# A hybrid decoder block on one core: the up-projection's first group prepares its inputs product by product

## The chip, the cores and the metric

The kernel runs on one core of a Trainium2 chip. A core has five engines, each with its own queue that it works off in order: TensorE for matrix products (PE, and PEld for its weight loads), VectorE (DVE), ScalarE (ACT), GpSimd (POOL) and SyncE (SP), which here only issues DMAs. The metric is the device time of one execution in microseconds (us). The number given is the median of three runs; the profile is of one further execution.

## The reference

The reference is one decoder layer on a sequence of 2048 tokens with width 1024, in float32. It is computed as follows.

```
n    = rms_norm(x, attn_norm_w)
proj = n @ w_in              # q, k, v, gate, a, b of DeltaNet; q, k, v, gate of retention
o    = concat(gated_deltanet(...), retention(...))      # 4 + 4 heads of 128
h    = x + o @ w_out
n2   = rms_norm(h, mlp_norm_w)
hdn  = causal_dwconv3(n2 @ w_up)                        # 1024 -> 2 * 2816
g, u = split(hdn)
h    = h + (silu(g) * u) @ w_down                       # 2816 -> 1024
out  = rms_norm(h, final_norm_w)
```

The DeltaNet heads carry a state from chunk to chunk, so that part is a chain of small matrix products, each waiting for a step on VectorE. The three big projections (w_out, w_up, w_down) have no such chain.

## The kernel before, in words

**Number format.** Every float32 matrix that is multiplied in a big projection is split into a rounded high part and the rest. `split` (L1123) does it in two instructions: an ACT copy into the rounded format (L1124) and a VectorE subtraction for the rest (L1125). `mm3` then makes one product out of three matmuls (L118, L119, L120): high by high, high by low, low by high.

**Seven products.** The projections use a scheme of the Strassen family: both operands are cut into 2 x 2 blocks, and seven block products numbered 1 to 7 take the place of eight. Four of the seven need a sum or difference of blocks on each side. In the up-projection the blocks of the input are b11, b12, b21, b22, and the products are used in the order 1, 2, 6, 7, 5, 4, 3. Product 1 takes b11, product 2 takes b21, product 3 takes b22; products 5, 6, 7 and 4 take the differences t1 = b12 - b11, t2 = b22 - t1, t3 = b22 - b12 and t4 = b21 - t2.

**Batches and passes.** The mixers (normalisation, input projection, DeltaNet, retention, output projection) work in four batches of 512 tokens, numbered 0 to 3. The up-projection works in two passes q = 0 and q = 1, each over two batches (1024 tokens); a pass goes through 22 groups g of output columns. Pass 0 reads the normalised rows n2d of batches 0 and 1 only, which lie in DRAM long before batch 3 is done. The up-projection is a generator (`mlp_up`, L1115 on). For q = 0 it loads the first group's weights (`load_w`, L1157, DMA at L1169, into the tiles "wur"; sums at L1176, splits into the tiles "wu"), then prepares the inputs (`prep_x`, L1130), then runs `group` (L1190) and, one group ahead, `load_w` of the next. `prep_x` takes one k tile at a time: it loads two rows of blocks into two raw tiles "xr" (L1138), makes four differences into "st" (L1146), and splits all seven operands into the tiles "x", before it goes to the next of the four k tiles. A product of a group is 4 k tiles x 3 matmuls = 12 matmuls of 128 x 512 (tile "p"), followed by an addition out of PSUM into "uc" (L1206 on VectorE, or a copy, L1226 and L1228 on ACT). `tail` does the convolution, the activation and the differences for the down-projection.

**What sets the order.** `ORDER` is a list of stage names written out by hand. A name begins with the batch; the rest says which stage: `pro` normalisation, `a`, `f`, `k0`, `q0`, `v0`, `kq` input projections, `dec` decays, `c`, `d`, `e`, `b`, `l` the preparation of DeltaNet chunks, `r00` to `r13` the recurrence (first digit the pair of heads, second the chunk; steps at L860 to L886), `h` and `y` retention, `P` products of the gate, `g` and `G` the gated mixing (L578 to L588), `W1` to `W7` the products of the output projection (weights "wv", loaded at L1061; the residual input "wx", L1045), and `N` the second normalisation (L1103), which writes n2d. A name that begins with `U` advances the up-projection's generator by one `yield`; the number behind the U has no meaning. Names of one stage may stand between those of another, so that their instructions mix. From this traced order the framework makes a fixed queue for each engine at compile time: at each point of a modelled run the engine takes the earliest traced instruction that is ready. The numbers of buffers per tile name (NXR, NUC, BUFS and others) limit how many of a name live at once.

**Fences.** `fence(k)` (L1127) puts the DMAs inside it, in the queue of SP, behind a certain earlier DMA: the last load of mixer weights ("c"), a load of batch 3's DeltaNet base ("z"), or a load of "wx" in batch 3 ("x"). Which one is read from a table, and where the named DMA has not been traced yet it is "c":

```
FX = (0, 2, 4, 1, 5)
FENCE = ["c", ("z", NB - 1, 0), ("z", NB - 1, 1), ("x", NB - 1, 0, 0), ("x", NB - 1, 1, 0), ("x", NB - 1, 2, 0), ("x", NB - 1, 3, 0)]
return tc.issue_after(marks.get(FENCE[FX[k]], marks["c"]).ins)
```

The first four entries of FX are for the input loads of the four k tiles, the fifth for the first group's weights.

## Time and profile before

| | before |
|---|---|
| runs, us | 2439.99, 2438.68, 2437.32 |
| median, us | 2438.68 |
| profiled execution, us | 2446.21 |
| its span, us | 2444.4 |
| TensorE busy in the span, us | 2389.4 |
| VectorE, ScalarE, GpSimd busy, us | 1658.3, 1075.1, 412.4 |
| mean granted TensorE clock | 0.991 |

The span reaches from the first to the last instruction of the profiled execution; the time is that of the whole execution. In lines of the profile, L and a number is a line of the kernel, `out<-in` names the tiles an instruction writes and reads, `x` and a number counts instructions, and a bracket at the end of a line gives how long the engine was idle before it and what ended that idle time. A granted clock of 1.00 is full speed.

### The profile page before, as it was taken

The numbers are of one execution on the slowest core, as the hardware profiler recorded it, in microseconds if no ns is written. First come the engines' busy times: TensorE is split into PE (matmuls) and PEld (weight loads), VectorE is DVE, ScalarE is ACT, GpSimd is POOL, SyncE is SP. The second block draws the span as 40 slices with busy tenths as digits, with TensorE's granted clock in tenths as the row PEclk, the third lists the DMA queues.
The fourth block names the chain that finished last, engine by engine and source line by source line (L and its number), as shares of the span: only waits on it lengthen the run. The fifth ranks groups of instructions, "written<-read, shape, count | busy, mean of one in ns | idle before, by whom it ended". The sixth has DMA issues, their size and how long they took to land.

```text
span 2444.4 us, 35994 instructions
## 1 busy us (share of the span) xinstructions
PE 2389.4 (98%) x12404; PEld 2010.2 (82%) x12404; DVE 1658.3 (68%) x3187; ACT 1075.1 (44%) x2286; POOL 412.4 (17%) x753
## 2 busy tenths in 40 slices
PE   8999899999999999998999999999999999999998
PEld 7887788878887888887788888888888888888887
DVE  6865686664744872667989988995556576554673
ACT  6744555555443662456544434442222234332341
POOL 1154113520043103140000000000000002431030
PEclk9999999999999999999999999999999999999999
DMA  8955789886777865697998878777668578774782
GB/s 317 379 195 181 290 316 357 309 335 229 277 265 223 321 234 173 208 339 272 351 343 320 301 283 311 290 261 255 241 229 319 198 272 281 251 223 144 229 253 99
DMA packets 307142, 652.40 MB, mean 267 GB/s; under 512 B 51024, under 2 KB 130320, under 8 KB 306960
## 3 DMA queue, kind: packets, MB, share of 16 engines
q1 hardware_dynamic: 290240, 635.80, 73.5%
q10 hardware_dynamic: 16720, 14.30, 1.9%
q8 instruction: 98, 1.61, 0.3%
q14 instruction: 84, 0.69, 0.1%
HBM read 444.12 MB, written 205.88 MB: 266 GB/s over the span
## 4 chain that ended last, share of the span: by engine, by line
PE 86%; DMA 4%; DVE 4%; POOL 3%; issue 2%; ACT 1%; SPq 0%; ACTq 0%; POOLq 0%; DVEq 0%
PE p L118 11%; PE p L119 11%; PE p L120 11%; PE d L120 6%; PE d L118 6%; PE d L119 6%; PE tok L539 3%; PE tok L540 3%; PE tok L541 3%; PE chm L119 3%; PE chm L118 3%; PE chm L120 3%; PE wo L120 2%; PE wo L118 2%; PE wo L119 2%
## 5 line engine op out<-in xcount | busy, mean ns | idle before, releaser
L119 PE MATMUL p<-x,wu 128*128 128x512 f32 x1176 | 457.8, 389 | 0.8 <-DVE x L1125 0.8
L118 PE MATMUL p<-x,wu 128*128 128x512 f32 x1176 | 452.8, 390 | 1.7 <-ACT uc L1226 1.3
L120 PE MATMUL p<-x,wu 128*128 128x512 f32 x1176 | 450.4, 389 | 0.0
L118 PEld LDWEIGHTS p<-x,wu 128*128 128x128 f32 x1176 | 220.7, 188 | 49.0 <-ACT uc L1226 1.7
L119 PEld LDWEIGHTS p<-x,wu 128*128 128x128 f32 x1176 | 220.7, 188 | 47.3 <-DVE x L1125 1.7
L120 PEld LDWEIGHTS p<-x,wu 128*128 128x128 f32 x1176 | 220.7, 188 | 45.8
L1253 DVE SCALAR_TENSOR_TENSOR acc<-uc,base,acc 128x1022 f32<-128x1022 f32 (+1 forms) x176 | 220.9, 1278 | 37.1 <-ACT acc L1250 36.9
L1206 DVE TENSOR_TENSOR uc<-p,uc 128x512 f32<-128x512 f32 x224 | 152.8, 685 | 135.1 <-PE p L120 129.6
L539 PE MATMUL tok<-wc,n 128*128 128x512 f32 (+2 forms) x576 | 196.9, 352 | 8.1 <-ACT n L449 5.7
L540 PE MATMUL tok<-wc,n 128*128 128x512 f32 (+2 forms) x576 | 200.2, 349 | 0.0
L541 PE MATMUL tok<-wc,n 128*128 128x512 f32 (+2 forms) x576 | 196.5, 349 | 3.1 <-DVE n L452 3.1
L184 POOL TENSOR_TENSOR vt<-vr 128x512 f32<-128x512 f32 x44 | 72.1, 1642 | 636.3 <-DMA vr<-in_w_d 458.9
L119 PE MATMUL d<-v,uu 128*128 128x512 f32 x448 | 174.3, 389 | 0.0
L120 PE MATMUL d<-v,uu 128*128 128x512 f32 x448 | 174.3, 389 | 0.0
L118 PE MATMUL d<-v,uu 128*128 128x512 f32 x448 | 174.3, 389 | 0.0
L118 PE MATMUL chm<-n,wc 128*128 128x512 f32 x384 | 153.1, 399 | 1.8 <-ACT og L583 1.8
L119 PE MATMUL chm<-n,wc 128*128 128x512 f32 x384 | 151.4, 394 | 0.0
L120 PE MATMUL chm<-n,wc 128*128 128x512 f32 x384 | 150.8, 393 | 0.0
L1250 ACT ACTIVATE acc<-uc,base 128x1024 f32<-128x1024 f32 x88 | 97.3, 1144 | 97.5 <-DVE uc L1206 49.5
L539 PEld LDWEIGHTS tok<-wc,n 128*128 128x128 f32 x576 | 109.8, 192 | 21.4 <-ACT n L449 5.9
L408 DVE SCALAR_TENSOR_TENSOR ca<-ca,base 128x511 f32<-128x511 f32 (+2 forms) x144 | 110.6, 768 | 21.6 <-ACT ca L405 21.1
L541 PEld LDWEIGHTS tok<-wc,n 128*128 128x128 f32 x576 | 108.6, 192 | 15.7 <-DVE n L452 3.3
(280 smaller groups left out, 5049.2 us busy)
## 6 DMA issues: line engine op xcount, KB each, us to landing
wu<-wu SPq DMA_DIRECT2D x308, 512.0 KB, 5.5
wc<-wd SPq DMA_DIRECT2D x116, 512.0 KB, 5.3
wv<-kW SPq DMA_DIRECT2D x112, 512.0 KB, 6.6
wc<-kP SPq DMA_DIRECT2D x84, 512.0 KB, 6.3
ur<-au SPq DMA_DIRECT2D x56, 512.0 KB, 5.7
wd<-wc SPq DMA_DIRECT2D x44, 512.0 KB, 6.6
wur<-in_w_u SPq DMA_DIRECT2D x44, 512.0 KB, 6.2
au<-st SPq DMA_DIRECT2D x88, 256.0 KB, 5.0
```

The costliest lines, as they stand in the source:

```text
L118: PE.matmul(ps, ah, bh, start=(first and i == 0), stop=False, skip_group_check=chk)
L119: PE.matmul(ps, ah, bl, start=False, stop=False, skip_group_check=chk)
L120: PE.matmul(ps, al, bh, start=False, stop=(i == n - 1), skip_group_check=chk)
L184: POOL.tensor_tensor(tt[:, j], a, b_, op=ALU.subtract)
L408: DVE.scalar_tensor_tensor(acc[:, s:], ps[:, :TB - s], w, acc[:, s:], op0=ALU.mult, op1=ALU.add)
L539: PE.matmul(ps, ah, wh, start=(k == 0), stop=False)
L540: PE.matmul(ps, ah, wl, start=False, stop=False)
L541: PE.matmul(ps, al_, wh, start=False, stop=(k == KT - 1))
L1206: add = lambda o, ps, a: DVE.tensor_tensor(o, ps, a, op=ALU.add)
L1250: ACT.activation(acc, u, AF.Copy, scale=mcw[:, ci, 2:3])
L1253: DVE.scalar_tensor_tensor(acc[:, t:], u[:, :T2 - t], w, acc[:, t:], op0=ALU.mult, op1=ALU.add)
```

## The change

The change has three parts.

First, for pass 0 the preparation of the inputs goes product by product. `first_x` loads all raw tiles, k tile by k tile, and splits the operand of product 1 only. `more_x(i)` prepares the operand of product i for all four k tiles; it writes t1 and t3 and t4 over raw blocks that are not needed any more, and t2 into "st". In the first group, `group` calls `more_x` for the next product ahead of each product, with a `yield` after each preparation and each product. Pass 1 keeps `prep_x`.

Second, with these yields the up-projection's first group takes 18 entries of the order instead of 11. The first of them moves from behind 3W3 to ahead of 3r10, and the others are spread between the entries of batch 3. A dozen other entries of the order move by one to three places.

Third, buffer numbers change: NUC 5 to 4, NPR 9 to 10, NXR 7 to 8, and in BUFS kv 8 to 7, NT 7 to 5, Cw 4 to 3, wvt 9 to 8, ca 11 to 12, rk 13 to 14, rq 2 to 4, rv 10 to 11.

```diff
@@ -21,7 +21,7 @@
 NVV = 23
 NWUR = 2
 NST = 4
-NUC = 5
+NUC = 4
 NACC = 8
 NWU = 9
 NWV = 5
@@ -29,27 +29,28 @@
 NU = 4
 NPB = 9
 NPM = 4
-NPR = 9
+NPR = 10
 NRAW = 3
 NLATE = 4
-NXR = 7
+NXR = 8
 FD = 6
-BUFS = {"n1": 8, "ykq": 4, "kv": 8, "NT": 7, "AT": 10, "o": 6, "n2s": 15, "xk": 2, "og": 1, "co": 6, "Cw": 4,
-        "wx": 1, "wsq": 5, "wvr": 2, "wvt": 9, "ca": 11, "mix": 5, "D": 6, "rk": 13, "rq": 2, "rv": 10, "sm": 5,
+BUFS = {"n1": 8, "ykq": 4, "kv": 7, "NT": 5, "AT": 10, "o": 6, "n2s": 15, "xk": 2, "og": 1, "co": 6, "Cw": 3,
+        "wx": 1, "wsq": 5, "wvr": 2, "wvt": 8, "ca": 12, "mix": 5, "D": 6, "rk": 14, "rq": 4, "rv": 11, "sm": 5,
         "sc": 15, "wg": 2, "kt": 4, "Ar": 2, "Nb": 6, "rot": 1, "rrow": 5}
 
-ORDER = ("0pro 0k0 0dec 0v0 0q0 0d0 0a0 0a1 0c0 0f0 0d1 0a2 0c1 0f1 0b0 0e0 0d2 0e1 0c2 0h0 0y0 0h1 0f2 "
-         "0d3 0a3 0c3 0l0 0e2 0O0 0y1 0f3 0r00 0r01 0e3 0r02 0r03 0O2 0kq 0b1 0l1 0O1 0r10 0r11 0p0 1pro "
-         "0O3 0h2 0Q0 0r12 0y2 0p1 0g0 1k0 0r13 0h3 0G0 1a0 0y3 0g1 1dec 0G1 1a3 1f0 1d0 1c0 1q0 0W1 0W2 "
-         "0W6 1d1 1a1 0W7 1f1 1c1 0W5 1v0 1e1 1d3 0Q2 0Q1 0W3 1f3 1d2 1b0 1h1 1e0 0Q3 1a2 0W4 1c3 1c2 1f2 "
+ORDER = ("0pro 0k0 0v0 0dec 0q0 0d0 0a0 0a1 0c0 0f0 0d1 0a2 0c1 0f1 0b0 0e0 0d2 0e1 0c2 0h0 0y0 0h1 0f2 "
+         "0d3 0a3 0c3 0l0 0O0 0y1 0f3 0r00 0e2 0r01 0e3 0r02 0r03 0O2 0kq 0b1 0l1 0O1 0r10 0r11 0p0 1pro "
+         "0O3 0h2 0Q0 0r12 0y2 0p1 0g0 1k0 0r13 0h3 0G0 0y3 1a0 0g1 1dec 0G1 1a3 1f0 1d0 1c0 1q0 0W1 0W2 "
+         "0W6 1d1 1a1 1c1 0W7 1f1 0W5 1v0 1e1 1d3 0Q2 0Q1 0W3 1f3 1d2 1b0 1h1 1e0 0Q3 1a2 0W4 1c3 1c2 1f2 "
          "1e2 1y1 1h0 1l0 1y0 1e3 0N 1r00 1r01 1b1 1r02 1S 1kq 1P1 1h2 1y2 1l1 1r03 1h3 1P4 1T 1P6 1P7 "
-         "1r10 1y3 1P5 1r11 2pro 1r12 2k0 1g1 1g0 2v0 1r13 1G1 2dec 1G0 2a0 2d1 1W1 1W2 2d0 2c0 2f0 1W6 "
-         "2a2 1W7 2d2 1W5 2f2 2c2 2a1 1W3 2e2 2e0 1W4 2c1 2f1 2q0 2d3 2e1 2b0 2a3 2h1 2y1 2c3 2b1 2h0 2f3 "
+         "1r10 1y3 2pro 1P5 1r11 1r12 2k0 1g1 1g0 2v0 1r13 1G1 2dec 1G0 2a0 2d1 1W1 1W2 2d0 2c0 2f0 1W6 "
+         "2a2 1W7 2d2 1W5 2f2 2a1 2c2 1W3 2e2 2e0 1W4 2d3 2c1 2f1 2q0 2a3 2e1 2b0 2h1 2y1 2c3 2b1 2h0 2f3 "
          "2e3 2l0 2P1 2r00 1N 2S 2kq 2r01 2P4 2T 2P6 2y0 2l1 2P7 2r02 2r10 2h2 2y2 2P5 2h3 3pro 2r03 2r11 "
          "2r12 3k0 2y3 2r13 2g1 2g0 3a0 3f0 2G0 3dec 3a1 2G1 3d0 2W1 2W2 3a2 3d1 2W6 3q0 3f1 3c1 2W7 3c0 "
-         "3e1 3b0 3d3 3v0 3h0 3e0 3y0 3h1 3d2 3c2 3y1 3kq 3f2 2W5 3a3 3e2 3c3 3f3 2W3 3b1 3l0 3e3 3S 3P1 "
-         "3r00 3r01 3P4 3h2 3T 3P6 3P7 3r02 3y2 3h3 3P5 3r03 3l1 3g0 3r10 3G0 3r11 3r12 3y3 2W4 2N 3g1 "
-         "3W1 3r13 3W2 3G1 3W6 3W7 3W5 3W3 U1 U2 U3 U4 3W4 3N U0 U6 U9 U7 U8 U5 U10")
+         "3e1 3b0 3d3 3v0 3h0 3d2 3e0 3y0 3h1 3c2 3y1 3kq 3f2 2W5 3e2 3a3 3c3 3f3 2W3 3b1 3l0 3e3 3S 3r00 "
+         "3r01 3P1 3P4 3h2 3T 3P6 3P7 3r02 3P5 3y2 3h3 3r03 3l1 3g0 U3 U1 U2 U4 3r10 3G0 3r11 U0 3r12 2W4 "
+         "U6 3y3 3g1 2N U7 U8 3W1 3r13 3W2 U9 3G1 3W6 3W7 3W5 3W4 3W3 U13 U17 U15 3N U12 U16 U5 U10 U11 "
+         "U14")
 P = 128
 S = 2048
 D = 1024
@@ -1154,6 +1155,47 @@
                 split(x_, src)
             yield
 
+    raws, t2s = {}, {}
+
+    def x_part(xc, i, kt, src):
+        x_ = xc[i, kt] = unit(xp, f"x{i}_{kt}", [P, 2, TB], F32R, bufs=1)
+        split(x_, src)
+
+    def first_x(xc):
+        for kt in range(4):
+            for i in range(2):
+                xr = raws[i, kt] = unit(up, "xr", [P, 2, TB], bufs=NXR)
+                k = 4 * i + kt
+                with fence(kt):
+                    for t in range(2):
+                        nc.sync.dma_start(xr[:, t], n2d[t, k // 2][k % 2])
+            x_part(xc, 1, kt, raws[0, kt][:, 0])
+            yield
+
+    def more_x(xc, i):
+        sub = lambda o, a, b_: DVE.tensor_tensor(o, a, b_, op=ALU.subtract)
+        for kt in range(4):
+            (b11, b12), (b21, b22) = ([raws[j, kt][:, t] for t in range(2)] for j in range(2))
+            if i == 2:
+                x_part(xc, 2, kt, b21)
+            elif i == 6:
+                sub(b11, b12, b11)
+                if kt % 2 == 0:
+                    t2s[kt // 2] = unit(up, "st", [P, 2, TB], bufs=NST)
+                t2 = t2s[kt // 2][:, kt % 2]
+                sub(t2, b22, b11)
+                x_part(xc, 6, kt, t2)
+            elif i == 7:
+                sub(b12, b22, b12)
+                x_part(xc, 7, kt, b12)
+            elif i == 5:
+                x_part(xc, 5, kt, b11)
+            elif i == 4:
+                sub(b21, b21, t2s[kt // 2][:, kt % 2])
+                x_part(xc, 4, kt, b21)
+            else:
+                x_part(xc, 3, kt, b22)
+
     def load_w(q, g):
         ws = {}
 
@@ -1187,7 +1229,7 @@
             nc.sync.dma_start(wud[g, i], ws[i].bitcast(F32))
         return ws
 
-    def group(q, g, ws, xc, st):
+    def group(q, g, ws, xc, st, ahead=None):
         f0, kind = g // 2, g % 2
         us = []
         for j in range(2):
@@ -1221,6 +1263,25 @@
             add(c21, ps[4], c21)
             add(c12, ps[5], c12)
             add(c12, ps[3], c12)
+        elif ahead is not None:
+            ps = {}
+            ids = (1, 2, 6, 7, 5, 4, 3)
+            for i, nx in zip(ids, ids[1:] + (None,)):
+                if nx:
+                    ahead(nx)
+                    yield
+                ps[i] = prod(i, ps[{2: 1, 3: 5}[i]] if i in (2, 3) else None)
+                if i < 3:
+                    ACT.activation(c12 if i == 1 else c11, ps[i], AF.Copy)
+                if i in (6, 3):
+                    add(c12, ps[i], c12)
+                if i == 7:
+                    add(c21, ps[i], c12)
+                if i == 5:
+                    add(c22, ps[i], c21)
+                if i == 4:
+                    add(c21, ps[i], c21)
+                yield
         else:
             p1 = prod(1)
             ACT.activation(c12, p1, AF.Copy)
@@ -1287,12 +1348,12 @@
         nxt = load_w(*gs[0])
     yield
     xc = {}
-    yield from prep_x(0, xc)
+    yield from first_x(xc)
     for n, (q, g) in enumerate(gs):
         ws = nxt
         if n + 1 < len(gs):
             nxt = load_w(*gs[n + 1])
-        parts = group(q, g, ws, xc, st)
+        parts = group(q, g, ws, xc, st, (lambda i: more_x(xc, i)) if n == 0 else None)
         while True:
             try:
                 next(parts)
```

## The prediction

> **What bounds the kernel now.** I read the page's busy shares and chain first, then the busy time by stretch, then a table of 4 us slices where TensorE is idle, and last the instructions in order of time there.
>
> ```profile
> span 2444.4 us, 35994 instructions
> PE 2389.4 (98%) x12404; PEld 2010.2 (82%) x12404; DVE 1658.3 (68%) x3187; ACT 1075.1 (44%) x2286; POOL 412.4 (17%) x753
> PE 86%; DMA 4%; DVE 4%; POOL 3%; issue 2%; ACT 1%; SPq 0%; ACTq 0%; POOLq 0%; DVEq 0%
> ```
>
> TensorE is busy for 98% of the span and carries 86% of the chain. All its work stays, so a change can only move the 55 us in which it is idle and the stretches in which its clock is low. Of these, two stretches early in the program and the passage from the last mixer batch to the up-projection matter here (columns: stretch, length, busy time of PE, PEld, DVE, ACT and POOL with counts, granted clock, DMA share, GB/s):
>
> ```profile
> 180.00:240.00 60.00, 53.99 (x417) 45.78 (x416) 33.27 (x71) 27.07 (x66) 27.66 (x68) 0.94 0.57 184
> 240.00:300.00 60.00, 54.20 (x344) 48.13 (x344) 36.16 (x108) 31.62 (x84) 8.10 (x7) 0.91 0.76 290
> ...
> 1100.00:1140.00 40.00, 31.86 (x264) 28.04 (x263) 25.53 (x69) 26.79 (x74) 3.03 (x3) 0.91 0.65 240
> 1140.00:1260.00 120.00, 117.62 (x534) 96.45 (x533) 107.69 (x170) 66.86 (x107) 7.82 (x12) 1.00 0.94 347
> ```
>
> The reader is to see 8.14 us of idle TensorE in 1100 to 1140, 2.38 us in the 120 us behind it, and that VectorE has 14.5 us free in the first stretch and only 12.3 in the second. The same 40 us in slices:
>
> ```profile
> 1100.00:1104.00 4.00, 2.54 (x57) 1.84 (x55) 3.05 (x7) 3.62 (x7) 0.00 (x0) 1.00 1.03 392
> 1104.00:1108.00 4.00, 1.68 (x21) 1.57 (x22) 3.87 (x9) 2.54 (x7) 0.00 (x0) 0.79 0.97 348
> 1108.00:1112.00 4.00, 4.00 (x25) 3.44 (x24) 0.83 (x3) 1.51 (x4) 0.00 (x0) 0.50 1.01 397
> 1112.00:1116.00 4.00, 4.00 (x33) 4.00 (x33) 2.45 (x7) 3.08 (x8) 0.00 (x0) 0.85 0.14 50
> 1116.00:1120.00 4.00, 3.52 (x32) 3.32 (x30) 2.73 (x8) 4.00 (x12) 0.00 (x0) 1.00 0.48 181
> 1120.00:1124.00 4.00, 2.57 (x18) 2.22 (x18) 2.71 (x8) 2.81 (x8) 0.00 (x0) 1.00 0.76 289
> 1124.00:1128.00 4.00, 3.39 (x30) 3.23 (x30) 2.71 (x10) 1.35 (x6) 1.01 (x1) 1.00 0.15 56
> 1128.00:1132.00 4.00, 3.56 (x25) 3.01 (x24) 2.12 (x5) 4.00 (x15) 0.00 (x0) 1.00 0.37 98
> ...
> 1136.00:1140.00 4.00, 2.60 (x15) 1.97 (x14) 2.61 (x9) 2.80 (x9) 1.01 (x1) 1.00 0.66 235
> ```
>
> There are three items. Two holes before 1108 (1.46 + 2.32 = 3.78 us). A low clock behind them: 0.21 of 1.68 busy us, 0.50 of 4.00 and 0.15 of 4.00, together 2.95 us lost. And small holes from 1116 on: 0.48 + 1.43 + 0.61 + 0.44 + 1.40 = 4.36 us. Why no up-projection product fills them is told by the order of time on TensorE, VectorE and the SP queue:
>
> ```profile
> 1104.83 1.15 PE L831 MATMUL yps<-NT 128*64 128x64 f32 x16 [2.29 <-DVE NT L824]
> 1107.46 1.08 PE L838 MATMUL ttps<-AT,pers 128*64 128x64 f32 x8 [1.49 <-ACT AT L827]
> ...
> 1145.34 0.39 PE L118 MATMUL p<-x,wu 128*128 128x512 f32 x1
> ...
> 1147.84 0.39 PE L120 MATMUL p<-x,wu 128*128 128x512 f32 x1
> ```
> ```profile
> 1141.93 0.68 DVE L1125 TENSOR_TENSOR wu<-wur,wu 128x512 fp32r<-128x512 f32 x1
> ```
> ```profile
> 1083.92 4.22 SPq L321 DMA_DIRECT2D wc<-kP  x3
> 1088.31 4.55 SPq L794 DMA_DIRECT2D AT<-z  x8
> ...
> 1093.91 7.34 SPq L1138 DMA_DIRECT2D xr<-n2d  x10
> 1101.60 2.33 SPq L1061 DMA_DIRECT2D wv<-kW  x4
> 1104.26 2.59 SPq L1138 DMA_DIRECT2D xr<-n2d  x4
> 1129.60 0.32 SPq L1061 DMA_DIRECT2D wv<-kW  x1
> 1130.09 0.33 SPq L1045 DMA_DIRECT2D wx<-in_x  x1
> 1130.53 0.37 SPq L1061 DMA_DIRECT2D wv<-kW  x1
> 1130.95 0.42 SPq L1169 DMA_DIRECT2D wur<-in_w_u  x1
> ```
>
> The first product begins at 1145.34, 3.4 us after its weight was split on VectorE at 1141.93. That weight's load went out at 1130.95 only: the SP queue issued nothing from 1106.85 to 1129.60, standing before a load of an output-projection weight (wv), and fence(4) puts the load of wur behind the wx load of the output projection's product 5, which is the one at 1130.09.
>
> **The change, part by part.** *Order of the inputs.* The work is the same: per input tile one ACT copy and one VectorE subtract for each of 28 splits, and 16 subtractions for the combinations. They now stand in the order in which the products use them: 4 splits for product 1, 4 for product 2, 8 subtractions and 4 splits for product 6, and so on. No instruction is added; two of the sums are written over their operands, so 2 units of "st" do what 8 did, while the 8 raw tiles stay until products 4 and 3 are prepared. Per VectorE operation:
>
> ```profile
> L1125 DVE TENSOR_TENSOR x<-xr,x 128x512 fp32r<-128x512 f32 x10 | 6.6, 687 | 1.0 <-ACT x L1124 0.9
> L873 DVE TENSOR_TENSOR pers<-wps,pers 128x256 f32<-128x256 f32 x4 | 1.7, 423 | 3.2 <-PE wps L870 3.2
> L880 DVE SCALAR_TENSOR_TENSOR pers<-pers,pers,sps 128x128 f32<-128x128 f32 x8 | 2.4, 342 | 1.4 <-PE sps L878 1.3
> L863 DVE SCALAR_TENSOR_TENSOR kv<-ks,pers,kv 128x128 f32<-128x128 f32 x6 | 1.8, 344 | 2.3 <-PE ks L860 2.2
> ```
>
> Before, product 1 stands in traced order behind all four groups of 4 subtractions and 7 splits. After, it needs 4 x splits and one weight split, 5 x 0.687 = 3.4 us of VectorE.
>
> *Place in the order.* The first entry of the up-projection moves from behind 3W3 to ahead of 3r10. At that point neither the product-5 nor the product-1 loads of batch 3 exist in the trace, so fence(4) and fence(2) fall back to "c", the last load of combined gate weights (wc at 1083.92). The two wur loads may then go out some 40 us earlier, ahead of the blocked wv load. They pass the wv loads at 1101.60 and 1129.60 and the wx load; 16 xr loads keep their place behind 1088. Products 1 and 2 are 12 matmuls each; from 1145.34 to 1147.84 there are 11 spacings of 0.227 us, so 2.7 us each and 5.45 us of filling that waits for nothing in batch 3. From 1145 on TensorE is full, so what is filled in before is saved at the end one for one.
>
> Holes from 1116 on: -4.4 us, all of them, since 5.45 is more than 4.36. Ends 0 and -4.4.
>
> Holes before 1108: how soon the x tiles land decides.
>
> ```profile
> DMA to landing us min/median/max: 2.7/6.2/8.2
> ```
> ```profile
> wur<-in_w_u SPq DMA_DIRECT2D x44, 512.0 KB, 6.2
> ```
>
> In issue order the first row of the fourth k tile is among the four xr loads at 1104.26, so it lands at about 1110; only the first k tiles can be multiplied by 1104. With the DMA share at 1.03 and 0.97 the two added wur loads (512 KB each, at 392 GB/s 1.3 us each) push these further. I take half of 3.78, -1.9; ends 0 and -3.8.
>
> Low clock: it follows the two early holes, so half of it goes with half of them, -1.5; ends 0 and -3.0. [...]
>
> From 1140 to 1260:
>
> ```profile
> 1169.80 0.50 PE L118 MATMUL p<-x,wu 128*128 128x512 f32 x1 [0.27 <-ACT x L1124]
> ...
> 1175.17 0.50 PE L119 MATMUL p<-x,wu 128*128 128x512 f32 x1 [0.77 <-DVE x L1125]
> ```
> ```profile
> PE p L118 <- ACT uc L1226: 1.3, 1, 1.3
> ```
>
> The two waits for x (1.0 us) go, as x is ready earlier; the wait of 1.3 us for the copy of product 1 out of PSUM, which product 2 adds to, is untouched. -1.0; ends 0 and -2.4.
>
> *What it costs.* VectorE work that lay behind 1141 moves into the recurrence of batch 3, whose steps L873, L880 and L863 stand 4, 4 and 3 times in the stretch. 11 weight and 8 combination operations at 0.60 us apart are 11.4 us, which the 14.5 free us take; VectorE is then 92% busy instead of 64%. A step that meets one waits half of 0.68 us on average, and 0.28 more of the 11 steps meet one: 11 x 0.28 x 0.34 = 1.1 us. +1.1; ends 0 and +7.5 (a whole operation ahead of each step). Behind a late step queue the mix products at L578, hence 3G1 and the output projection 3W.
>
> *The 17 other moves and the caps.* 0v0, 0e2, 0y3, 1c1, 2pro, 2a1, 2d3, 2a3, 3d2, 3e2, 3P1, 3P5 and the rest move by one to three places. Where TensorE is full they can neither win nor lose; only 0y3 lies in a stretch with much idle time (180 to 300, 11.8 us), and its own hole there is this:
>
> ```profile
> PE ro L992 <- DVE o L883: 1.1, 1, 1.1
> ```
>
> I take 0, with ends -1.1 and +1.1. Caps: NT 7 to 5, kv 8 to 7, wvt 9 to 8: in the traced order a batch's heads use four NT and four kv units, and the next batch's "c" entries stand behind the levels and the last recurrence step that free them, so the cover is that order, and I take 0. Cw 4 to 3 serves four tiles that live together and so cannot act as written. NUC 5 to 4 leaves two groups of two tiles; a group lasts 84 x 0.227 = 19 us, which covers its tail. If such a cover fails, the price is a hole like the largest ones above, 1.5 to 2.3 us for each.
>
> Sum: -4.4 - 1.9 - 1.5 - 1.0 + 1.1 = -7.7 us. The profiled execution took 2446.2 us (span 2444.4 and 1.8 around it), 7.5 above the median of the runs; I take the difference over unchanged: 2438.68 - 7.7 = 2431.0.
>
> **Rivals.** *First: the inputs come no earlier.* The wur loads stay behind the blocked wv load, for want of free units or because their traced place gives them no priority. For it speaks that the xr loads, fenced only behind 1083.92 and 1088.31, went out at 1093.91; against it, that ten of them went out long before the block. Only the late x waits go: -1.0, 2437.7.
>
> *Second, slower: preparation in front of the recurrence.* Operations of 0.68 us stand ahead of each of the 11 steps, and the chain of batch 3 is 7.5 us later. Products 1 and 2 fill 5.45 us; product 6 needs 12 more VectorE operations, 7.2 us. It decides from the point where the chain's delay passes what the two products fill: -5.4 + 7.5 = +2.1, and with one more fall of the clock as measured, +3.0, it is +5.1: 2443.8. For it speaks VectorE at 107.69 of 120 us behind 1140, against it the 14.5 free us. [...]
>
> *Third: everything is filled.* All holes and the low clock go with no cost: -4.4 - 3.8 - 3.0 - 2.4 - 1.1 = -14.7, 2424.0.
>
> **How the numbers follow.** About 0.2% (4.9 us) is what a measurement of this kernel can tell from no change. The forecast has 0.44, the third rival 0.10, the first 0.25, the second 0.21. Faster by over 0.2% is below 2433.8: forecast and third rival, 0.54; the first gives "same", 0.25; the second, 0.21. The range reaches from the third rival to just short of the second, 2424 to 2443.5; the likeliest case's own range is 2426 to 2434.
>
> **What would show it.** After: p matmuls begin before 1120 rather than at 1145; wur is issued before 1106; idle TensorE in the 40 us before the first group's end falls from 8.1 to under 3; the slice with clock 0.50 is shorter. The recurrence steps L873 to L863 keep their pace. The prediction is wrong if p still begins at about 1140, if the last recurrence of batch 3 ends over 5 us later, or if idle time grows in the first three batches, whose order I took as free.

## The result and the profile after

| | before | after |
|---|---|---|
| runs, us | 2434.62 to 2440.91 (8 runs) | 2441.88 to 2454.00 (8 runs) |
| median, us | 2438.98 | 2449.99 |
| profiled execution, us | 2446.21 | 2450.48 |
| its span and mean clock | 2444.4, 0.991 | 2448.5, 0.991 |

The changed kernel is slower by 11.0 us by the medians. The ratio here and below is that of the runs as a whole, so it is not exactly that of the medians: 1.0042, 95% interval 1.0031 to 1.0053. The prediction was 2431.0, with a range up to 2443.5. Both the sign and the range missed.

The page of the changed kernel begins like this (span, busy time by engine, chain):

```profile
span 2448.5 us, 35996 instructions
PE 2388.8 (98%) x12404; PEld 2006.8 (82%) x12404; DVE 1656.8 (68%) x3187; ACT 1075.2 (44%) x2286; POOL 426.0 (17%) x753
PE 82%; DMA 6%; DVE 4%; POOL 3%; issue 2%; ACT 1%; SPq 1%; ACTq 0%; POOLq 0%; DVEq 0%
```

In the changed kernel `mm3` is L119 to L121, `split` L1125 and L1126, and the copy L824 of before is L825. TensorE's busy time is the same to 0.6 us. TensorE's matmuls are the same, so its idle time and what a low clock costs are where to look. Here are the stretches of the passage, now after the change, and one earlier stretch:

```profile
420.00:480.00 60.00, 57.07 (x381) 47.94 (x380) 34.02 (x98) 30.25 (x96) 30.89 (x72) 1.00 0.84 288
...
1100.00:1140.00 40.00, 29.81 (x194) 24.68 (x193) 32.44 (x78) 24.15 (x68) 4.42 (x3) 0.87 0.69 270
...
1140.00:1260.00 120.00, 116.32 (x525) 94.96 (x524) 94.37 (x151) 64.31 (x103) 11.59 (x12) 0.97 0.89 331
```

Idle TensorE in 1100 to 1140 is 10.19 us instead of 8.14, behind 1140 it is 3.68 instead of 2.38, and the mean clocks are 0.87 and 0.97 instead of 0.91 and 1.00. Outside this passage, 420 to 480 is the only stretch with over 1 us more idle time than in the profile of before (2.93 us, against 0.74). The slices that answer to the prediction's, with those in which a second low clock shows:

```profile
1100.00:1104.00 4.00, 1.60 (x5) 0.45 (x3) 3.97 (x8) 3.67 (x6) 0.00 (x0) 0.77 1.04 406
1104.00:1108.00 4.00, 1.97 (x16) 1.78 (x16) 3.94 (x9) 3.02 (x8) 0.00 (x0) 0.50 1.05 410
1108.00:1112.00 4.00, 3.47 (x22) 2.93 (x23) 3.52 (x7) 1.49 (x3) 0.00 (x0) 0.50 1.03 419
...
1144.00:1148.00 4.00, 2.01 (x7) 0.81 (x5) 4.00 (x8) 4.00 (x9) 0.00 (x0) 0.82 0.86 332
1148.00:1152.00 4.00, 3.35 (x8) 2.60 (x9) 4.00 (x7) 2.09 (x5) 0.00 (x0) 0.50 0.59 214
1152.00:1156.00 4.00, 4.00 (x16) 3.19 (x15) 4.00 (x10) 1.99 (x4) 0.00 (x0) 0.83 0.87 302
```

The reader is to see VectorE (third number) at 3.97 and 3.94 of 4 us just where TensorE stands still, and again from 1144 on. In order of time on TensorE (start, duration, line, tiles; in brackets the idle time ahead and what ended it):

```profile
1098.44 0.50 PE L119 MATMUL p<-x,wu 128*128 128x512 f32 x1
1099.53 0.50 PE L120 MATMUL p<-x,wu 128*128 128x512 f32 x1 [0.58 <-DVE x L1126]
...
1102.05 0.69 PE L120 MATMUL p<-x,wu 128*128 128x512 f32 x1 [1.58 <-DVE x L1126]
...
1104.17 1.97 PE L832 MATMUL yps<-NT 128*64 128x64 f32 x16 [1.00 <-DVE NT L825]
1108.53 1.09 PE L839 MATMUL ttps<-AT,pers 128*64 128x64 f32 x8 [2.39 <-issue]
...
1146.42 0.69 PE L119 MATMUL wo<-wv,wu 128*128 128x512 f32 x1 [0.87 <-ACT wu L1069]
...
1148.65 0.79 PE L120 MATMUL p<-x,wu 128*128 128x512 f32 x1 [1.11 <-DVE x L1126]
```

The first product does begin 47 us earlier (1098.44 for 1145.34). But it waits for its own inputs, and so does batch 3's `yps`. Why is told by VectorE's queue of the changed kernel at that time:

```profile
1098.19 0.68 DVE L1218 TENSOR_TENSOR st<-st,wur 128x512 f32<-128x512 f32 x1
1098.79 0.68 DVE L1126 TENSOR_TENSOR x<-xr,x 128x512 fp32r<-128x512 f32 x1
1099.51 0.69 DVE L527 TENSOR_TENSOR mix<-P,mix 128x512 f32<-128x512 f32 x1
1100.11 1.89 DVE L1126 TENSOR_TENSOR x<-xr,x 128x512 fp32r<-128x512 f32 x3
1101.92 0.68 DVE L527 TENSOR_TENSOR mix<-P,mix 128x512 f32<-128x512 f32 x1
1102.52 0.68 DVE L1126 TENSOR_TENSOR x<-xr,x 128x512 fp32r<-128x512 f32 x1
1103.12 0.69 DVE L1218 TENSOR_TENSOR st<-wur,st 128x512 f32<-128x512 f32 x1
1103.83 0.48 DVE L825 COPY NT<-ttps 32x128 f32<-32x128 f32 x2
...
1107.29 0.68 DVE L1126 TENSOR_TENSOR wu<-st,wu 128x512 fp32r<-128x512 f32 x1
1108.01 0.77 DVE L835 COPY pers<-yps 64x256 f32<-64x256 f32 x2
```

The copy at 1103.83 is the step of batch 3's chunk preparation (stage 3l1, the "levels": products of small triangular blocks, each copied out of PSUM before the next) that `yps` waits for. Seven operations of the first group and two of the mixer stand ahead of it; it starts 5.6 us after the first of them. The next copy of the levels, L835 at 1108.01, stands in the same way behind first-group work, the last of it the split at 1107.29. It copies what `yps` made (done at 1106.14) and `ttps` begins at 1108.53, so the wait of 2.39 us, for which the profile names no releaser ("issue"), is of the same kind. The kernel before has such splits there too, but fewer: four ahead of its copy L824 at 1104.49.

Behind 1120 the output projection of batch 3 is what came late. The matmuls of tile "wo" alone, in the same stretch, before the change and after it (columns: stretch, length, busy TensorE with count, clock, DMA share, GB/s):

```profile
1120.00:1145.00 25.00, 11.83 (x47) 1.00 0.62 224
```
```profile
1120.00:1145.00 25.00, 3.26 (x12) 1.00 0.40 149
```

The first group's products (tile "p") ran for 4.66 us in this stretch, where there were none before, and the output projection lost 8.57 us there. So the early products took the place of output-projection work rather than of holes, and that work stood later between waits for ACT and VectorE (the rows at 1146.42 and 1148.65), with a second fall of the clock.

### The profile page after: what moved, and what is told of

It is laid out like the page before. It is cut to its first block, busy times and chain, and to the rows that moved or that the text cites. A ratio compares the mean times of both kernels' runs of the same rounds, so it can differ in the third digit from the quotient of the medians.

```text
span 2448.5 us, 35996 instructions
## 1 busy us (share of the span) xinstructions
PE 2388.8 (98%) x12404; PEld 2006.8 (82%) x12404; DVE 1656.8 (68%) x3187; ACT 1075.2 (44%) x2286; POOL 426.0 (17%) x753
## 4 chain that ended last, share of the span: by engine, by line
PE 82%; DMA 6%; DVE 4%; POOL 3%; issue 2%; ACT 1%; SPq 1%; ACTq 0%; POOLq 0%; DVEq 0%
PE p L120 11%; PE p L121 11%; PE p L119 11%; PE d L120 6%; PE d L121 6%; PE d L119 6%; PE chm L121 3%; PE chm L119 3%; PE chm L120 3%; PE tok L540 3%; PE tok L541 3%; PE tok L542 3%; PE wo L121 2%; PE wo L119 2%; PE wo L120 2%
## 5 line engine op out<-in xcount | busy, mean ns | idle before, releaser
L119 PE MATMUL p<-x,wu 128*128 128x512 f32 x1176 | 454.2, 390 | 1.7 <-ACT x L1125 1.7
L121 PE MATMUL p<-x,wu 128*128 128x512 f32 x1176 | 451.7, 390 | 0.0
L119 PEld LDWEIGHTS p<-x,wu 128*128 128x128 f32 x1176 | 220.9, 188 | 47.6 <-ACT x L1125 2.2
L121 PEld LDWEIGHTS p<-x,wu 128*128 128x128 f32 x1176 | 221.1, 188 | 45.6
L119 PE MATMUL d<-v,uu 128*128 128x512 f32 x448 | 174.3, 389 | 0.0
L121 PE MATMUL d<-v,uu 128*128 128x512 f32 x448 | 174.3, 389 | 0.0
L119 PE MATMUL chm<-n,wc 128*128 128x512 f32 x384 | 152.0, 396 | 1.8 <-ACT og L584 1.8
L121 PE MATMUL chm<-n,wc 128*128 128x512 f32 x384 | 150.7, 392 | 0.0
L1311 ACT ACTIVATE acc<-uc,base 128x1024 f32<-128x1024 f32 x88 | 97.3, 1143 | 89.5 <-DVE uc L1248 43.2
```

What stands on the lines that cost most here:

```text
L119: PE.matmul(ps, ah, bh, start=(first and i == 0), stop=False, skip_group_check=chk)
L121: PE.matmul(ps, al, bh, start=False, stop=(i == n - 1), skip_group_check=chk)
L1311: ACT.activation(acc, u, AF.Copy, scale=mcw[:, ci, 2:3])
```

## The experiments

All runs at a glance. "Passage" is 1080 to 1260 us. Idle is 180 less the busy time of TensorE in it. "Half" is the number of 3.41 us windows in which the granted clock was 0.50 there (the last section shows that it comes in such windows). Both are from one profiled execution. For the kernel before there are two: idle 10.5 with 2 windows, and 9.6 with none (span 2430.2, a second profiled execution with a time of 2431.95, label e8). The kernel before was timed again beside each set of runs, and each ratio is to its own set; the medians of before lie between 2437.2 and 2439.0, so medians of different sets compare to within some 2 us.

| run | what it is | median, us | ratio to before [95%] | idle, us | half |
|---|---|---|---|---|---|
| after | the change | 2449.99 | 1.0042 [1.0031, 1.0053] | 14.5 | 5 |
| e1 | after, entries U late | 2462.98 | 1.0113 [1.0088, 1.0139] | 22.3 | 8 |
| e2 | before, entries U early | 2472.47 | 1.0151 [1.0130, 1.0171] | 31.2 | 14 |
| e3 | before, new buffer numbers | 2443.39 | 1.0023 [1.0014, 1.0032] | 13.9 | 1 |
| e4 | before, new mixer order | 2445.29 | 1.0033 [1.0019, 1.0046] | 13.8 | 7 |
| e5 | after, old mixer order and numbers | 2453.60 | 1.0076 [1.0060, 1.0093] | 19.3 | 6 |
| e6 | after, old mixer order | 2453.52 | 1.0070 [1.0055, 1.0085] | 19.2 | 8 |
| e7 | after, old numbers | 2446.85 | 1.0039 [1.0024, 1.0054] | 14.6 | 5 |
| e9 | before, weights early | 2448.22 | 1.0044 [1.0029, 1.0059] | 13.7 | 2 |
| e10 | after, only product 1's inputs early | 2445.24 | 1.0030 [1.0015, 1.0045] | 11.6 | 5 |
| e11 | after, weight stores on ACT's queue | 2455.10 | 1.0073 [1.0058, 1.0088] | 20.0 | 7 |
| e12 | after, 20 x splits on GpSimd | 2449.72 | 1.0049 [1.0034, 1.0064] | 17.6 | 5 |
| e13 | after, product 1 behind 3r12 | 2447.77 | 1.0040 [1.0025, 1.0055] | 16.8 | 4 |
| e14 | e9, first group behind 3r12 | 2444.19 | 1.0024 [1.0014, 1.0034] | 12.8 | 3 |
| e15 | e13, and the other products behind 3W | 2453.03 | 1.0058 [1.0046, 1.0070] | 21.7 | 7 |
| e16 | after, preparation behind the levels | 2452.90 | 1.0058 [1.0045, 1.0071] | 20.5 | 8 |
| e17 | before, preparation behind the levels | 2435.73 | 0.9989 [0.9980, 0.9997] | 9.4 | 0 |
| e18 | e9, preparation behind the levels | 2443.65 | 1.0025 [1.0015, 1.0034] | 10.6 | 3 |

### Which part costs: e1 to e8

e1 puts the 18 entries of the new group late, where the old ones were; e2 puts the 11 entries of the old group early.

```diff
 e1, the end of the order of the changed kernel
-... 3l1 3g0 U3 U1 U2 U4 3r10 3G0 3r11 U0 3r12 2W4 U6 3y3 3g1 2N U7 U8 3W1 3r13 3W2 U9 3G1 3W6 3W7 3W5 3W4 3W3 U13 ...
+... 3l1 3g0 3r10 3G0 3r11 3r12 2W4 3y3 3g1 2N 3W1 3r13 3W2 3G1 3W6 3W7 3W5 3W4 3W3 U0 U1 U2 U3 3N U4 U5 ... U17
 e2, the end of the order of the kernel before
-... 3l1 3g0 3r10 3G0 3r11 3r12 3y3 2W4 2N 3g1 3W1 3r13 3W2 3G1 3W6 3W7 3W5 3W3 U1 U2 U3 U4 3W4 3N U0 ...
+... 3l1 3g0 U0 U1 U2 3r10 3G0 3r11 U3 3r12 3y3 2W4 U4 2N U5 3g1 3W1 3r13 3W2 U6 3G1 3W6 3W7 3W5 3W3 U7 U8 3W4 3N U9 U10
```

> The changed kernel, but all 18 entries of the up-projection stand where the 11 stood before: four behind 3W3, the rest behind 3N. Preparation stays product by product, caps and other moves stay. Theory P (the loss comes from the early place of the first group, whose inputs and products then stand in the queues of VectorE, SP and TensorE ahead of batch 3's recurrence and output projection): the 11 us go, 2436 to 2441, and idle TensorE between 1080 and 1200 falls from 14.5 to about 9 us. Theory R (the loss comes from the caps and the other moves, or from the product-by-product code itself): it stays at 2446 to 2452.

> The kernel before with its own code (row group by row group), caps and mixer order, but its 11 up-projection entries are moved to the early places: three behind 3g0, one each behind 3r11, 2W4, 2N and 3W2, two behind 3W3 and two behind 3N. Theory P: slower by 5 to 12 us, 2444 to 2451, with p matmuls beginning before 1120. Theory R: within 3 us of before.

Measured: 2462.98 and 2472.47, both outside every range that was expected. Late entries with the new code, order and numbers are 13 us worse than the change itself, so it isn't simply "early is bad". A late entry does not keep VectorE from running its work early, as the compile-time order takes the earliest traced instruction that is ready. In e1's trace TensorE waits 2.71 us in the recurrence for the step L863 at 1109.12, which stands behind a split of the first group (L1125 at 1108.51), while the first product begins at 1148.71 only. Early entries with the old preparation are 34.5 us slower than before, and the change's product-by-product code, with its 18 entries, is worth some 19 us against that (compare e5, which has the same old mixer order and numbers but for NXR: 2453.60).

e3 and e4 make the other two parts alone, in the kernel before.

```diff
 e3
-NUC = 5
+NUC = 4
-NPR = 9
+NPR = 10
-NXR = 7
+NXR = 8
 and the eight numbers of BUFS as in the change
 e4
 the fifteen moves of mixer entries as in the change, and behind them
+... 3W1 3r13 3W2 3G1 3W6 3W7 3W5 3W4 3W3 U0 U1 U2 U3 3N U4 U5 U6 U7 U8 U9 U10
```

> The kernel before with the changed buffer numbers alone (NUC, NPR, NXR and BUFS). Theory P: within 3 us of before, 2436 to 2442. Theory R in its form 'caps': slower by 5 us or more, with new holes in the first three batches, where NT, kv and wvt are used.

> The kernel before with the changed places of the mixer stages alone (0v0, 0e2, 0y3, 1c1, 2pro, 2a1, 2d3, 2a3, 3d2, 3e2, 3P1, 3P5, 2W4, 3g1, 3W4); the up-projection's 11 entries stay behind 3W3 and 3N. Theory P: within 3 us of before. Theory R in its form 'moves': slower by 5 us or more, with new holes in batches 0 to 2.

Measured: +5.4 us for the numbers (interval 1.0014 to 1.0032), +7.4 us for the moves. Both were costed at 0 in the prediction. The rival of these two runs expected new holes in the first three batches; instead most of the loss lies in the passage: 3.4 and 3.3 us more idle than the larger value of before, and 1 and 7 windows at half clock. Which move and which number does it was not tested. For e4 TensorE's largest wait in the passage is at the head of the output projection (its lines are one lower than before's):

```profile
1144.98 0.50 PE L117 MATMUL wo<-wv,wu 128*128 128x512 f32 x1 [3.57 <-ACT wu L1067]
```

e5, e6 and e7 undo the same parts in the changed kernel: both (NXR stays 8, which the new code needs), the moves alone, the numbers alone.

```diff
 e6, and with the numbers of before also e5
-... 3r00 3r01 3P1 3P4 3h2 3T 3P6 3P7 3r02 3P5 3y2 3h3 ...
+... 3P1 3r00 3r01 3P4 3h2 3T 3P6 3P7 3r02 3y2 3h3 3P5 ... (all mixer entries as before, the U entries early)
 e7
-NUC = 4
+NUC = 5
 and NPR and BUFS as before
```

> The changed kernel with its product-by-product code, its 18 up-projection entries at the early places and NXR at 8, but with the other buffer numbers and the mixer order of before. Theory A (the parts add up: caps +5.4 and moves +7.4 as measured alone, so the regrouped, early first group is itself a gain of about 2 us): 2433 to 2440. Theory I (the parts depend on each other: the early first group only does no more harm than 11 us because the moves and caps make room for it): 2450 or more, with idle TensorE between 1080 and 1260 above the 14.5 us of the changed kernel.

> The changed kernel with the mixer stages in the order of before; the up-projection's entries stay early and the caps stay changed. Theory A: 7 us less than the changed kernel, 2441 to 2445. Theory I: no less than the changed kernel, 2448 to 2460.

> The changed kernel with the buffer numbers of before except NXR, which stays at 8. Theory A: 5 us less than the changed kernel, 2442 to 2447. Theory I: no less than the changed kernel, 2448 to 2460.

Measured: 2453.60, 2453.52, 2446.85. With the early group present, undoing the moves costs 3.5 us more. Undoing the numbers wins 3.1 by the medians, but the ratios, 1.0039 and 1.0042, have almost the same interval, so that no effect of the numbers is shown there. So the early group alone costs 16 us, the moves alone 7, the numbers alone 5, and all three together 11. The parts do not add up: the moves pay back part of what the early group costs.

> The kernel before once more, for a second profile of it. Its first profiled execution was 7.5 us above its median and lost 21 us to a low clock. If that is chance from one execution to the next, idle TensorE is again 53 to 56 us in all and 9 to 11 us between 1080 and 1260, while the loss by the clock differs by some us, and the time is 2434 to 2441. If the profile lengthens every execution of this kernel, the time is again 2445 to 2448.

e8 is the kernel before once more, for a second trace: 2431.95 us, span 2430.2, with TensorE busy for 2378.9 us at a mean clock of 0.996. The profiled execution on which the prediction stands was busy for 2389.4 at 0.991. The same matmuls thus took 10.5 us less of TensorE's time, as the clock was low for less of it, and idle time was 51.2 us instead of 55.0. Of what was expected, idle time in all (53 to 56 us) and the time (2434 to 2441) came out lower, and the passage (9.6 us) inside its range; that the profile itself lengthens the run is not borne out by this execution.

### Which piece of the early group costs: e9 to e12

e9 lets only the first group's weight loads go early, in the kernel before.

```diff
-FX = (0, 2, 4, 1, 5)
+FX = (0, 2, 4, 1, 0)
```

> The kernel before with one number changed: the fifth entry of FX is 0, so that the first group's weight loads are fenced behind the last mixer weights, as in the changed kernel, and no longer behind wx. Order, caps and code stay. The prediction's mechanism (weights that come earlier let products 1 and 2 fill the holes of batch 3): 2431 to 2436. Theory Q (first-group work that the compile-time order puts ahead of batch 3's output projection waits for its tiles at the head of TensorE's in-order queue and delays the projection's own operands on ACT and VectorE): slower, 2442 to 2455.

Measured: 2448.22, as slow as the whole change. Nothing but one fence was moved, and the first product begins at 1100.41:

```profile
1100.41 0.47 PE L118 MATMUL p<-x,wu 128*128 128x512 f32 x1 [3.94 <-DVE mix L526]
```
```profile
1096.30 0.69 DVE L1176 TENSOR_TENSOR st<-wur 128x512 f32<-128x512 f32 x1 [2.35 <-DMA wur<-in_w_u]
...
1099.58 0.69 DVE L526 TENSOR_TENSOR mix<-P,mix 128x512 f32<-128x512 f32 x1
```

The profile names the mixer's addition L526 as what ended the wait. On VectorE it stands behind five operations of the first group, and the first of these had held VectorE up for 2.35 us, until its weights landed.

So early weights are by themselves enough for a loss of this size. What the prediction took as the gain is the price.

e10 keeps the change but leaves only the first five entries early, the weights and the splits for product 1; e11 takes the stores of the first two groups' split weights out of SP's queue; e12 takes the VectorE half of the splits of products 6, 7, 5, 4 and 3 to GpSimd.

```diff
 e10
+... 3l1 3g0 U0 U1 U2 U3 3r10 3G0 3r11 U4 3r12 2W4 3y3 3g1 2N 3W1 ... 3W4 3W3 U5 U6 U7 3N U8 ... U17
 e11
-            nc.sync.dma_start(wud[g, i], ws[i].bitcast(F32))
+            (nc.scalar if g < 2 else nc.sync).dma_start(wud[g, i], ws[i].bitcast(F32))
 e12
-        split(x_, src)
+        split(x_, src, POOL if i in (6, 7, 5, 4, 3) else DVE)
```

> The changed kernel with the loads and the splits of product 1 at the early places (four entries behind 3g0, one behind 3r11), and all later entries, the next weights and the products and their preparation, behind 3W3 (three) and 3N (ten). Theory Q: 4 us or more less than the changed kernel if the preparation of products 2 and 6 is what delays batch 3, 2440 to 2446; if product 1 alone is what stands in the way, no change, 2447 to 2453.

> The changed kernel with the DRAM stores of the first two groups' split weights issued from ACT's queue instead of SP's. Theory S (these stores, waiting for their splits in SP's in-order queue, hold up the wv and wx loads behind them until 1150): 4 us or more less than the changed kernel, 2440 to 2446, with the wv load of 1150.55 some 20 us earlier. Theory Q: within 3 us of the changed kernel, or slower by what ACT loses.

> The changed kernel with the low parts of x for products 6, 7, 5, 4 and 3 (20 subtractions) on GpSimd, which is idle there, instead of VectorE. If VectorE's load in front of the output projection is the cause: 4 us or more less than the changed kernel, 2440 to 2446. If it is the waiting at the head of TensorE's queue for x: slower, 2452 to 2465, since a subtraction of this size takes 1.64 us on GpSimd against 0.68 on VectorE.

Measured: 2445.24, 2455.10, 2449.72. Holding the later entries back wins 4.8 us of the 11 by the medians and 3.0 against the run of before beside it; the two intervals overlap. On ACT's queue the stores are worse, with a wait of 5.64 us for an x tile behind them, and the wv load of 1150.55 comes no earlier: it goes out at 1154.95, behind loads of the next weights. So e11 does not test what a free SP queue would be worth. But in the changed kernel only 0.2 us of TensorE's waits between 1100 and 1200 are put down to a wv load. Taking the later splits off VectorE changes nothing in sum, though GpSimd takes longer for them (four took 8.87 us there, with a hole of 3.61 us behind it at 1146), so this run does not clear VectorE.

### Where TensorE waits: e13 to e15

These put the matmuls of the first group behind a matmul of batch 3 in TensorE's queue: product 1 behind the last one of 3r12 (e13), the whole first group of e9 likewise (e14), and in the changed kernel product 1 behind 3r12 and the rest behind the last traced "wo" (e15).

```diff
+    def behind(q, g, i):
+        return tc.issue_after(marks["r", NB - 1, 2].ins) if (q, g) == (0, 0) and i == 1 else nullcontext()
...
-            mm3(ps, ...)
+            with behind(q, g, i):
+                mm3(ps, ...)
```

> The changed kernel, with product 1's matmuls of the first group put behind the last matmul of batch 3's recurrence step 3r12 in TensorE's queue; loads, splits and places stay. Theory Q1 (product 1, standing at the head of the in-order queue while its x tiles land, opens the holes and the low clock at 1098 to 1112): the waits of p for x before 1105 (0.58 and 1.58 us) go, idle plus clock loss in 1080 to 1200 falls by 3 to 6 us, 2443 to 2447. Theory Q2 (the loss is in the operands of the output projection, late on ACT and VectorE behind the preparation): 2447 to 2453.

> The kernel before with the weight loads early (FX's fifth entry 0, +11 us alone) and, besides, all matmuls of the first group put behind the last matmul of 3r12 in TensorE's queue. Theory Q1: the wait of 3.9 us and the low clock go, and what remains is a gain from filling: 2434 to 2441. Theory Q2: 2444 to 2452, as with the early weights alone.

> The changed kernel with product 1 behind 3r12's last matmul and products 2 to 3 of the first group each behind the last output-projection matmul traced so far. Theory Q1 for the second cluster of holes (1143 to 1152, p waiting for x of product 6): those waits (0.66 and 1.11 us) go too, 2440 to 2445. Theory Q2: TensorE stands before output-projection operands instead, 2447 to 2456.

Measured: 2447.77, 2444.19, 2453.03, all three in or at the range of theory Q2. In the trace of e13, with no product in the way, TensorE waits longer, and for VectorE:

```profile
1106.35 1.97 PE L832 MATMUL yps<-NT 128*64 128x64 f32 x16 [5.12 <-DVE NT L825]
```

e14 has 4.74 us at the same place and e15 again 5.12. So the waits of product 1 in the changed kernel (0.58 + 1.58) had lain inside the wait for the levels. In e14 the early weights cost 5.8 us, against 11.0 in e9 (the intervals just overlap), so there the products in TensorE's queue may be up to half of the loss; in e13, for product 1 of the changed kernel, no such gain shows. A product at the head of TensorE's queue is thus at most part of the cause; the first cluster of holes comes from VectorE.

### Preparation behind the levels: e16 to e18

Here the first group's VectorE and ACT work is issued behind the last copies of batch 3's levels, in the changed kernel, in the kernel before, and in e9. In the changed kernel (e16) this holds for the weights and for products 1, 2 and 6 alone; products 7, 5, 4 and 3 keep their freedom. In e17 and e18 it holds for all seven.

```diff
+    def levels(on=True):
+        s = ExitStack()
+        for m in ("lv", "la") if on else ():
+            s.enter_context(tc.issue_after(marks[m, NB - 1].ins))
+        return s
...
-            x_part(xc, 1, kt, raws[0, kt][:, 0])
+            with levels():
+                x_part(xc, 1, kt, raws[0, kt][:, 0])
...
-    with fence(4):
+    with fence(4), levels():
         nxt = load_w(*gs[0])
```

> The changed kernel with one difference: every VectorE and ACT operation that prepares the first group's x tiles and weights is issued behind the last copies of batch 3's levels (L842 on VectorE, L828 on ACT). Nothing is added or left out. Theory (first hole cluster is batch 3's levels chain waiting on VectorE behind first-group preparation): the copy out of ttps goes back to within 2.5 us of its transposes, the waits of yps and ttps together are under 3 us, the clock does not fall below 0.8 before 1116, and the time falls by 4 to 7 us against the changed kernel, to 2443 to 2446 (ratio to before 1.002 to 1.0035). Products 1 and 2 begin at about 1108 rather than 1098. Rival (the levels are not what the time hangs on; the first group's place in TensorE's own queue is): the same time as the changed kernel, 2447 to 2452, with the idle time moved behind 1116. What this cannot mend in either theory is the second cluster at 1140 to 1160, some 4 us.

> The kernel before with the same difference alone: the first group's VectorE and ACT preparation behind batch 3's levels, its order row group by row group and its entries as before. Theory (levels chain on VectorE): before too has some first-group operations ahead of the copy at L824, which is what its 2.29 us wait is made of; the wait shrinks to about 1 us, the low clock behind it goes, and the time is 2 to 5 us below before, 2433 to 2437. Rival (before's wait at yps is the length of the chain itself): no change, 2437 to 2440. If the preparation then comes late for the product at 1145, up to 4 us slower.

> The kernel of e9 (before with only the loads of the first group's weights allowed early, 1.0044) with the first group's VectorE and ACT preparation behind batch 3's levels. Theory (levels chain on VectorE): most of e9's loss goes, 2438 to 2443. Rival (the loss is the products standing ahead of batch 3's output projection in TensorE's queue): 2446 to 2450, as e9.

Measured: 2452.90, 2435.73 and 2443.65. e17 came out as the theory said and e18 just above its range: e18 keeps 6.4 of e9's 11 us, and e17 is 1.6 us faster than before, the one version that beats both kernels, though by less than can be told from no change by the bound used here. In e17's trace the levels hardly wait, where before had 2.29 and 1.49 us (e18's waits are the same 0.46 and 0.57):

```profile
1097.09 1.15 PE L831 MATMUL yps<-NT 128*64 128x64 f32 x16 [0.46 <-DVE NT L824]
1098.81 0.65 PE L838 MATMUL ttps<-AT,pers 128*64 128x64 f32 x8 [0.57 <-ACT AT L827]
```

e16 missed: 2443 to 2446 was expected, and it is as slow as ever. Its trace tells why (TensorE first, then VectorE):

```profile
1096.29 1.44 PE L832 MATMUL yps<-NT 128*64 128x64 f32 x16 [3.47 <-DVE NT L825]
1098.29 1.09 PE L839 MATMUL ttps<-AT,pers 128*64 128x64 f32 x8 [0.56 <-ACT wu L1125]
...
1110.72 2.08 PE L861 MATMUL ks<-pers,ykq 128*128 128x128 f32 x8 [2.72 <-DVE pers L881]
...
1138.45 0.45 PE L581 MATMUL mxt<-base,mix 128*128 128x128 f32 x1 [8.10 <-DVE mix L579]
```
```profile
1095.22 0.69 DVE L1126 TENSOR_TENSOR x<-xr,x 128x512 fp32r<-128x512 f32 x1 [1.99 <-ACT x L1125]
1095.95 0.48 DVE L825 COPY NT<-ttps 32x128 f32<-32x128 f32 x2
...
1106.13 1.87 DVE L1126 TENSOR_TENSOR x<-xr,x 128x512 fp32r<-128x512 f32 x3
1107.93 1.88 DVE L1183 TENSOR_TENSOR xr<-xr 128x512 f32<-128x512 f32 x3
1109.74 0.67 DVE L1228 TENSOR_TENSOR st<-st,wur 128x512 f32<-128x512 f32 x1
1110.34 0.59 DVE L881 SCALAR_TENSOR_TENSOR pers<-pers,pers,sps 128x128 f32<-128x128 f32 x2
...
1134.19 1.28 DVE L1126 TENSOR_TENSOR wu<-wur,wu 128x512 fp32r<-128x512 f32 x2
```

The levels' last wait is down to 0.56 us (2.39 in the changed kernel), but `yps` still waits 3.47 us. Its copy L825 stands behind a split that was left free, and VectorE stood idle for 1.99 us in front of that split (inferred, as the trace gives no numbers of products: of those left free only product 3's splits read a loaded block as it is). The rest of the preparation now stands ahead of the recurrence (L881 at 1110.34, behind nine of its operations from 1104.59 on) and ahead of the gated mixing (L579 at 1137.96), where TensorE has nothing to do for 8.10 us. From the recurrence's last step L884 at 1131.72 to L579 it takes 6.2 us; before, the same way took 2.7 (1136.00 to 1138.66). Most of the wait moved from one chain step of batch 3 to the next ones. That the first cluster comes from preparation ahead of the levels is shown by e17 and e18, where all of it is behind them; e16 is not a clean test of it. That the levels alone are the cause of the 11 us is not borne out: e18 keeps more than half of its loss with the levels free. In these traces what costs is preparation on VectorE and ACT ahead of a step of batch 3's chain, at the levels, in the recurrence or at the mixing, wherever the order puts it.

What stays open: how much of the second cluster (1143 to 1149 in the changed kernel) is due to ACT and how much to VectorE, which are both fully busy from 1144 to 1148. No run took the two apart. Open is also what a free SP queue would be worth, and how the moves and the numbers cost what they cost.

## Why the prediction was wrong

**Place in the order: right.** The weight loads went out early and the products could begin early. The SP queue of the changed kernel:

```profile
1088.26 0.85 SPq L1211 DMA_DIRECT2D wur<-in_w_u  x2
...
1133.43 12.50 SPq L1229 DMA_DIRECT2D wu<-wu  x4
1150.55 0.32 SPq L1062 DMA_DIRECT2D wv<-kW  x1
```

The loads are at 1088.26 (1130.95 before), and p begins before 1120 as named. The first rival falls with that. The block in SP's queue did not go away: the stores of the split weights now stand in it, and the next wv load goes out behind them, at 1150.55.

**Holes from 1116 on, -4.4: the step that failed.** "Products 1 and 2 ... 5.45 us of filling that waits for nothing in batch 3" took matmuls as free to fall into any hole. They stand at a fixed place in TensorE's queue, wait there for their own splits, and those splits stand ahead of batch 3 on VectorE. e9, which makes this step alone, is 11.0 us slower where a gain was forecast. From 1116 to 1140 there are 4.78 us of holes after (24 less 19.22 busy), against 4.37 before.

**Holes before 1108, -1.9, and low clock, -1.5.** Both came out with the other sign. From 1096 to 1116 idle is 5.99 us after and 3.77 before, and there are three windows at half clock there instead of two, and two more behind 1146. The prediction let half of the clock loss go with half of the holes. Product 1's matmuls did run there, for 1.25 us in the window ahead of the fall, and the clock fell all the same.

**From 1140 to 1260, -1.0.** The waits for x grew rather than went: idle is 3.68 us for 2.38, since the output projection has been pushed between the products.

**What it costs, +1.1 (0 to +7.5): the second step that failed.** The pricing asked only how the recurrence would fare, and the recurrence kept its pace (its last step L884 runs at 1133.58; before, L883 at 1136.00). The same argument was not made for the levels, 10 us earlier, nor for the output projection behind. VectorE's "14.5 free us" were an average over 40 us: at the levels it was busy 15.39 of 16 us (1096 to 1112), with 11.65 before.

**The other moves and the caps, 0: a term put at nothing.** Alone they cost 7.4 and 5.4 us (e4, e3); in the change the moves win 3.5 (e6), and no effect of the numbers is shown (e7). Fifteen mixer entries moved, by up to four places, not 17 or a dozen by up to three; and three of the four combinations (t1, t3, t4) are written over their operands, not two. Neither count enters the sum.

**The rivals.** The second, preparation in front of batch 3's chain with one more fall of the clock, came nearest (2443.8): its mechanism is the one found, while its place (the recurrence) is right only for e16 and e1; in the changed kernel the delay came at the levels and behind 1143. That no step passes a split ahead of it is what the traces show. In those of before and after, all 3187 VectorE instructions, 1943 activations on ACT, 753 GpSimd instructions and 1532 DMAs of SP began in the order of the built program (by line), and so did 12276 of TensorE's 12404 matmul records; the other 128 are of two neighbouring groups of small matmuls (L819 and L821 of before) that interleave. In the changed kernel the copy at 1103.83 reads matmuls that had ended by 1098.6, and starts only behind the operation at 1103.12.

In sum: in the passage, the changed kernel has 4.4 us more idle time than the mean of the two executions of before (14.5 against 10.1) and 3 to 5 more windows at half clock, which cost about 1.7 us each (an estimate, half of 3.41) where TensorE is fully busy and less where it also waits. Worked from the busy time in those windows the loss is 6.3 us against 2.8 and 0, so 4.9 us more than the mean. Together that is 9.3 us; 420 to 480 has 2.2 more. This is a comparison of single executions and not an exact account of the 11.0 us: outside the passage the clock cost 8.5 us after the change, and 14.8 and 7.5 in the two of before.

## What to carry to other kernels

Work that is moved forward in fixed queues, which the engines worked off in order here (the counts are with the rivals above), is ahead of every chain step that it passes on every engine, not only the one that comes to mind. Before calling it a filler, list what stands behind it on VectorE and ACT over the next few microseconds, slice by slice and not on average. A filler has to be ready when it reaches the head of the queue (in e9 VectorE stood still for 2.35 us in front of one whose weights had not landed), and its preparation is best put behind the chain's own operations, as in e17. In this order neither the buffer numbers nor the moves by a few places were free, and the costs of the parts did not add.
